# A new place on ScalarE for 100 weight negations and 8 weight casts, and another buffer order for the gate's weights

## The chip, the cores and the metric

The kernel is one program on one core of a Trainium2 chip. The metric is the device time of one execution in microseconds. Before the change it is 2661.06 us, the median of 3 runs (2660.25 to 2668.28).

## The reference, cut to what matters

The kernel computes two layers of a decoder trunk for one sequence of 1024 tokens, width 1024, in float32.

```python
def reference(x, ...):
    h = x
    for layer in range(DEPTH):                       # DEPTH = 2
        gains = norm_gains[layer]
        hn = rmsnorm(h, gains[0])
        if layer % 2 == 0:
            mix = mixer_ab(hn, w_in_ab[0], ...)      # gated DeltaNet + mLSTM, one output projection
        else:
            mix = mixer_c(hn, positions, w_qkv_c[0], ...)  # attention in a window of 128
        h = h + rmsnorm(mix, gains[1])
        hn = rmsnorm(h, gains[2])
        ff = jnp.square(jax.nn.relu(hn @ w_up[layer])) @ w_down[layer]   # 1024 -> 4096 -> 1024
        h = h + rmsnorm(ff, gains[3])
        gate = jax.nn.sigmoid(h @ w_ple_gate[layer])
        h = h + gate * (p[layer] @ w_ple[layer])
    return h
```

`rmsnorm` divides by the root of the mean square over the 1024 channels, so it needs a sum over the partitions. Inside the mixers each head projects q, k, v (and gates), and `mixer_c` scores 128 queries at a time against 256 keys.

## The kernel before

**Layout and weights.** Activations lie as channels by tokens, in two halves of 512 tokens (`h` = 0, 1; HT = 512). A matmul multiplies a 128 x 128 piece of a weight with 128 x 512 of activations. To keep float32 precision, every weight block of 128 x 8 x 128 is held as two float32r tiles, a high and a low half (names end in h and l), and a product is three matmuls: high by high, high by the activation's low half, low by high (lines 109 to 111 in `mm3`, lines 831 to 833 in `product`). One block by one half of the tokens is 24 matmuls.

The two halves are made by `wsplit` in three steps: POOL issues a DMA that loads the high half; ScalarE writes the negative of what landed into the low half (line 102, called the *negation* here); POOL issues a second DMA that adds the weight from memory onto it (line 103). So the low half is complete one negation and one transfer after the high half has landed. `raw_block` does it without the second transfer: a plain load, a cast on ScalarE, a subtraction on VectorE (`split`, line 145).

**Buffers.** Blocks from the pool "w" have 4 buffers for high and 4 for low halves. In the MLP's pool a tag "wd" has 8 buffers of either kind; `block` takes "w" where the index modulo 8 is under 4, else "wd". PSUM has 3 banks for the blocks ("mm"), 2 each for "s1" and "s2", 1 for "s3". The small tiles of the tag "sq" have 4 buffers.

**Order.** A scheduler orders the list of each engine by its own cost estimates when the program is built; every engine then works through its list in order, and an instruction whose input is not there holds up all that stand behind it on that engine.

**The stages of a layer, with the names that are used later:**

- *Projections of the mixer.* Layer 0: `proj` makes 28 blocks, each used for both halves of the tokens (48 matmuls). Layer 1: `roped` and `project` make 24 blocks named pq and pv, each used for one half (weights wqq000 and on, wqk01, wv10), with the scores of attention between them (ps and sc, lines 1193 and 1200). Their evictions are four copies on ScalarE (line 1103, tiles rs), the casts of q come at line 1109, the sum of the rotated parts at line 1133.
- *Output projection* (`out_proj`): 8 blocks wo00 to wo07 (layer 1: wo10 to wo17), first for half 0, then for half 1. Product mo, eviction into mix, a square moq, a running sum mos on VectorE (line 759). While half 1 is being multiplied, half 0 is normalized twice: pn00ps and mr00ps are matmuls with a matrix of ones that sum the squares over the partitions (`rstd`, line 116). The squares for mr00ps are mn00q (line 133, ScalarE), and their running sum is mn00s (lines 138 and 140, VectorE). The first digit is the layer, the second the half of the tokens.
- *MLP up* (`up`): 16 blocks wa00 to wa015 (layer 1: wa10 to wa115), a scheme of Strassen's kind that saves one product in eight. Block p gives product pa (4 of the 8 pieces), copied by ScalarE to sp and stored to s_dram, and product pb; their sum c gets a Relu and a square on ScalarE (lines 844 and 845) and is stored to r_dram, both stores issued by ScalarE (lines 846, 858). Blocks 12 to 15 are raw blocks. The squares of half 1 (mn01q) and the sums pn01ps and mr01ps lie among the first blocks. Then come further products from recombined weights (A, S).
- *MLP down*: products dn, in several groups; it ends with the layer's last norm.
- *Gate* (`ple`): 8 blocks wg000 to wg007 (half 0; also layer 1: wg100 and on), product pg, eviction a Tanh.

These are the lines of the split, of which everything here speaks:

```python
nc.gpsimd.dma_start(out=hi, in_=src)
nc.scalar.mul(lo, hi.bitcast(F32), -1.0)
nc.gpsimd.dma_start(out=lo, in_=src, accum_op=ALU.add)
```

Of the kernel before, what the change touches and what calls it, by code (L numbers as in the profile page):

```python
# [56 lines left out]
class Trunk:  # L57
    def __init__(self, ctx, tc, io):
        self.ctx, self.tc, self.nc, self.io = ctx, tc, tc.nc, io
        nc = self.nc  # L60
        self.cp = ctx.enter_context(tc.tile_pool(name="cp", bufs=1))
        self.bigp = ctx.enter_context(tc.tile_pool(name="bigp", bufs=4))
        self.wp = ctx.enter_context(tc.tile_pool(name="wp", bufs=4))
        self.dp = ctx.enter_context(tc.tile_pool(name="dp", bufs=1, space=DRAM))
        self.ps = ctx.enter_context(tc.tile_pool(name="ps", bufs=2, space=PSUM))
        cp = self.cp
        self.lead = self.ple_load(0, 0), self.ple_weight(0, 0)
        self.cst = cp.tile([P, C_HEAD], F32, name="cst")
        nc.sync.dma_start(out=self.cst, in_=io["cst"][:, 0:C_HEAD])
        self.par = cp.tile([P, G_N], F32, name="par")  # L70
        nc.sync.dma_start(out=self.par, in_=io["par"])
        self.row = cp.tile([P, R_N], F32, name="row")
        nc.sync.dma_start(out=self.row, in_=io["row"].partition_broadcast(P))
        self.ident = self.cst[:, C_ID:C_ID + P]
        self.ones = self.cst[:, C_ONE:C_ONE + P]
        self.epsc = cp.tile([P, 1], F32, name="epsc")
        nc.vector.memset(self.epsc, EPS)
        self.h_dram = self.dp.tile([2, 2, 2, P, KT, HT], F32, name="h_dram")
        self.pw_dram = self.dp.tile([2, 2, KT, P, HT], F32, name="pw_dram")
        self.mix_dram = self.dp.tile([KT, P, T], F32, name="mix_dram")  # L80
# [14 lines left out]
    def wsplit(self, src, tag, name, pool=None, n=KT, tags=None, **kw):  # L95
        nc = self.nc
        pool = pool or self.wp
        th, tl = tags or (tag + "h", tag + "l")
        hi = pool.tile([P, n, P], F32R, tag=th, name=name + "h", **kw)
        lo = pool.tile([P, n, P], F32R, tag=tl, name=name + "l", **kw)  # L100
        nc.gpsimd.dma_start(out=hi, in_=src)
        nc.scalar.mul(lo, hi.bitcast(F32), -1.0)
        nc.gpsimd.dma_start(out=lo, in_=src, accum_op=ALU.add)
        return hi, lo
# [220 lines left out]
    def proj(self, blk, hn, name):  # L325
        w = self.wsplit(self.io["w_in"][blk], "w", name)
        out = []
        for h in range(2):
            ps = self.mmps(f"{name}{h}")
            self.mm3(ps, w, hn[h])  # L330
            out.append(ps)
        return out
# [14 lines left out]
    def conv_silu(self, pool, out, ps, ch, name):  # L347
        nc = self.nc
        x = pool.tile([P, T], F32, tag="pre", name=name + "x", bufs=3)
        for h in range(2):  # L350
            nc.scalar.copy(x[:, h * HT:(h + 1) * HT], ps[h])
# [159 lines left out]
    def head_a_gate(self, pool, hd, hn):  # L511
        nc = self.nc
        n = f"a{hd}"
        gate = pool.tile([P, T], F32, tag="gate", name=n + "gate", bufs=2)
        for h, ps in enumerate(self.proj(hd * 4 + 3, hn, n + "z")):
            g = gate[:, h * HT:(h + 1) * HT]
            nc.scalar.activation(g, ps, AF.Tanh, scale=0.5)
            nc.vector.scalar_tensor_tensor(g, g, 1.0, ps, ALU.add, ALU.mult)
        return gate
# [49 lines left out]
    def head_b_in(self, pool, hd, hn):  # L569
# [5 lines left out]
        for dst, blk, s in ((kq[:, 0, :], 1, 1.0), (kq[:, 1, :], 0, P ** -0.5), (vT, 2, 1.0)):  # L575
            for h, ps in enumerate(self.proj(base + blk, hn, f"{n}{blk}")):
                nc.scalar.activation(dst[:, h * HT:(h + 1) * HT], ps, AF.Copy, scale=s)
        gate = pool.tile([P, T], F32, tag="gate", name=n + "gate", bufs=2)
        for h, ps in enumerate(self.proj(base + 3, hn, n + "og")):
            nc.scalar.activation(gate[:, h * HT:(h + 1) * HT], ps, AF.Tanh, scale=0.5)  # L580
# [139 lines left out]
    def block(self, mp, i, src, name):  # L720
        if i % 8 < 4:
            return self.wsplit(src, "w", name)
        return self.wsplit(src, "wd", name, pool=mp, tags=("wd", "wd"), bufs=8)

    def raw_block(self, mp, src, name, pool, tags, **kw):
# [4 lines left out]
        self.split(hi, lo, raw)  # L730
        return hi, lo

    def out_proj(self, src, w, layer, old, bias):
# [7 lines left out]
        def step(h, c):  # L741
# [4 lines left out]
            if h == 0:  # L746
                wts.append(self.block(mp, c, w[c], f"wo{layer}{c}"))
            ps = self.mmps(f"mo{layer}{h}{c}")
            self.mm3(ps, wts[c], src[h])
            if bias is None:  # L750
                nc.scalar.copy(acc[:, c, :], ps)
            else:
                nc.scalar.activation(acc[:, c, :], ps, AF.Identity, bias=bias[:, c:c + 1])
# [81 lines left out]
    def up(self, mp, layer, x11, x21, n1, later):  # L835
# [13 lines left out]
        for p in range(NP):  # L849
            if p < NP - 4:  # L850
                w = self.block(mp, p, wu[p], f"wa{layer}{p}")
            else:
                w = self.raw_block(mp, wu[p], f"wa{layer}{p}", mp, ("wd", "wd"), bufs=8)
# [3 lines left out]
            nc.scalar.copy(s, ps)  # L857
# [128 lines left out]
    def ple(self, mp, layer, acc, n0):  # L986
# [12 lines left out]
        for h in range(2):  # L999
            a = acc[h]  # L1000
            for c in range(KT):
                n = f"{layer}{h}{c}"
                if h == 0:
                    wts.append(self.block(mp, c, self.io["w_gate"][layer, c], "wg" + n))
# [5 lines left out]
                nc.scalar.activation(th, ps, AF.Tanh, scale=0.5)  # L1010
# [60 lines left out]
    def mixer_c(self, hn, norm, proj):  # L1071
# [5 lines left out]
        with tc.tile_pool(name="att", bufs=1) as pool:  # L1077
# [16 lines left out]
            def roped(h, blk, dst, name):  # L1094
                sl = slice(h * HT, (h + 1) * HT)
                w = self.wsplit(self.io["w_qkv"][blk], "w", "wq" + name)
# [4 lines left out]
                for b in range(4):  # L1101
                    o, i = slice(32 * b, 32 * b + 32), slice(32 * (b ^ 1), 32 * (b ^ 1) + 32)
                    nc.scalar.copy(xs[o], ps[i])
# [8 lines left out]
            def project(h, kt):  # L1112
# [9 lines left out]
                w = self.wsplit(self.io["w_qkv"][10 + kt], "w", f"wv{h}{kt}")  # L1122
# [3 lines left out]
                nc.scalar.activation(x, ps, AF.Identity, bias=self.par[:, G_BQKV + 10 + kt:G_BQKV + 11 + kt])  # L1126
# [211 lines left out]
```

## Time and profile before

| what | value |
|---|---|
| median of 3 runs | 2661.06 us (2660.25 to 2668.28) |
| the profiled execution | 2662.71 us |
| its span (first to last instruction) | 2660.9 us |
| mean granted clock of TensorE in it | 0.978 of full speed |
| TensorE matmuls (PE), weight loads (PEld) | 94%, 76% of the span |
| VectorE, ScalarE, POOL | 55%, 39%, 11% |
| memory traffic | 150 GB/s over the span |

All durations are from one execution, which took 1.65 us more than the median. A time in a row is in us from the start of the span. In a row of waits or in brackets behind an instruction, the name behind the arrow is what the waiting instruction was released by, as the profile infers it. A matmul row may stand for several instructions (x2). "PEclk" is the granted clock of TensorE in a stretch, 1.00 for full speed.

### The profile page before, as it was taken

The numbers are of one execution on the slowest core, as the hardware profiler recorded it, in microseconds if no ns is written. First come the engines' busy times: TensorE is split into PE (matmuls) and PEld (weight loads), VectorE is DVE, ScalarE is ACT, GpSimd is POOL, SyncE is SP. The second block draws the span as 40 slices with busy tenths as digits, with TensorE's granted clock in tenths as the row PEclk, the third lists the DMA queues.
The fourth block names the chain that finished last, engine by engine and source line by source line (L and its number), as shares of the span: only waits on it lengthen the run. The fifth ranks groups of instructions, "written<-read, shape, count | busy, mean of one in ns | idle before, by whom it ended". The sixth has DMA issues, their size and how long they took to land.

```text
span 2660.9 us, 31154 instructions
## 1 busy us (share of the span) xinstructions
PE 2502.4 (94%) x11541; PEld 2018.9 (76%) x11541; DVE 1466.9 (55%) x2768; ACT 1050.5 (39%) x1986; POOL 298.8 (11%) x405
## 2 busy tenths in 40 slices
PE   6999999999879999999999989968899999999999
PEld 4778878877668887888877766736678887888877
DVE  4788763252667763233366677763578751333373
ACT  5343333253465444211134666633465443211141
POOL 2111111111100001111021211001100000111120
PEclk9999999999989999999999999988999999999999
DMA  8443444466876457555445754216875456655543
GB/s 245 100 98 88 103 107 115 112 181 153 241 248 214 162 166 206 145 140 153 117 125 145 188 129 96 64 52 170 233 233 206 155 166 184 152 142 143 123 130 111
DMA packets 137223, 401.77 MB, mean 151 GB/s; under 512 B 24944, under 2 KB 25840, under 8 KB 132720
## 3 DMA queue, kind: packets, MB, share of 16 engines
q0 software_dynamic: 53920, 188.90, 31.8%
q1 hardware_dynamic: 51024, 166.84, 18.1%
q10 hardware_dynamic: 32128, 44.05, 4.6%
q8 instruction: 91, 1.49, 0.2%
q14 instruction: 60, 0.49, 0.1%
HBM read 321.16 MB, written 78.58 MB: 150 GB/s over the span
## 4 chain that ended last, share of the span: by engine, by line
PE 56%; issue 11%; DMA 6%; DVE 3%; ACT 2%; POOL 2%; POOLq 0%; SPq 0%; ACTq 0%; DVEq 0%
PE dn L831 8%; PE dn L833 8%; PE dn L832 8%; PE S L833 3%; PE S L831 3%; PE S L832 3%; PE pg L111 2%; PE pg L110 2%; PE pg L109 2%; PE po L1222 2%; PE mo L111 1%; PE mo L110 1%; PE mo L109 1%; PE A L833 1%; PE A L831 1%
## 5 line engine op out<-in xcount | busy, mean ns | idle before, releaser
L953 DVE TENSOR_TENSOR ff<-ff,dn 128x512 f32<-128x512 f32 x224 | 150.8, 684 | 318.1 <-PE dn L833 318.0
L831 PE MATMUL S<-xt,h 128*128 128x512 f32 x384 | 149.4, 389 | 0.0
L832 PE MATMUL S<-xt,h 128*128 128x512 f32 x384 | 149.4, 389 | 0.0
L833 PE MATMUL S<-xt,l 128*128 128x512 f32 x384 | 149.1, 389 | 0.0
L940 DVE TENSOR_TENSOR hid<-hid 128x1024 fp32r<-128x1024 f32 x64 | 75.8, 1221 | 125.5 <-ACT hid L939 125.5
L939 ACT CAST hid<-hid 128x1024 fp32r<-128x1024 f32 x64 | 64.2, 1045 | 96.7 <-DMA hid<-r_dram 77.4
L844 ACT ACTIVATE c<-c 128x512 f32<-128x512 f32 x64 | 40.3, 630 | 113.6 <-DVE c L917 88.0
L832 PEld LDWEIGHTS S<-xt,h 128*128 128x128 f32 x384 | 72.1, 188 | 15.0
L833 PEld LDWEIGHTS S<-xt,l 128*128 128x128 f32 x384 | 72.1, 188 | 15.0
L831 PEld LDWEIGHTS S<-xt,h 128*128 128x128 f32 x384 | 72.1, 188 | 14.9
L759 DVE TENSOR_TENSOR mos<-mos,moq 128x512 f32<-128x512 f32 x28 | 19.3, 688 | 92.8 <-ACT moq L755 92.6
L1209 ACT ACTIVATE sc<-sc,sm 128x128 f32<-128x128 f32 x128 | 49.8, 390 | 50.8 <-DVE sm L1206 36.3
L1222 PE MATMUL po<-pt,vt 128*128 128x512 f32 x120 | 61.1, 634 | 7.4 <-DVE pt L1220 4.1
L882 ACT CAST h<-r 128x1024 fp32r<-128x1024 f32 x32 | 33.6, 1050 | 73.5 <-DVE r L881 38.7
L1193 PE MATMUL ps<-kh,q 128*128 128x256 f32 (+1 forms) x128 | 38.7, 328 | 17.6 <-DVE sc L1200 10.7
L1013 DVE SCALAR_TENSOR_TENSOR pth<-pth,ppw 128x512 f32<-128x512 f32 x32 | 21.6, 687 | 56.4 <-ACT pth L1010 53.5
L831 PE MATMUL A<-xt,h 128*128 128x512 f32 x128 | 49.8, 389 | 0.0
L832 PE MATMUL A<-xt,h 128*128 128x512 f32 x128 | 49.8, 389 | 0.0
L833 PE MATMUL A<-xt,l 128*128 128x512 f32 x128 | 49.8, 389 | 0.0
L831 PE MATMUL S<-xb,s 128*128 128x512 f32 x128 | 49.8, 389 | 0.0
L832 PE MATMUL S<-xb,s 128*128 128x512 f32 x128 | 49.8, 389 | 0.0
L833 PE MATMUL S<-xb,s 128*128 128x512 f32 x128 | 49.8, 389 | 0.0
(3068 smaller groups left out, 7764.4 us busy)
## 6 DMA issues: line engine op xcount, KB each, us to landing
r<-w_up SPq DMA_DIRECT2D x64, 512.0 KB, 4.7
hid<-r_dram SPq DMA_DIRECT2D x32, 1024.0 KB, 7.9
r_dram<-c ACTq DMA_DIRECT2D x64, 256.0 KB, 2.9
pw_dram<-pwo SPq DMA_DIRECT2D x16, 512.0 KB, 3.8
h_dram<-mix SPq DMA_DIRECT2D x16, 512.0 KB, 4.4
s_dram<-sp ACTq DMA_DIRECT2D x32, 256.0 KB, 4.1
s<-s_dram SPq DMA_DIRECT2D x32, 256.0 KB, 2.8
r_dram<-s ACTq DMA_DIRECT2D x32, 256.0 KB, 4.7
```

The lines of the kernel that those rows point to most:

```text
L109: mm(ps, w[0][:, k, :], a[0][:, k, :], start=k == 0, stop=False)
L110: mm(ps, w[0][:, k, :], a[1][:, k, :], start=False, stop=False)
L111: mm(ps, w[1][:, k, :], a[0][:, k, :], start=False, stop=k == n - 1)
L831: mm(ps, wh, x[0][:, k, :], start=k == 0, stop=False)
L832: mm(ps, wh, x[1][:, k, :], start=False, stop=False)
L833: mm(ps, wl, x[0][:, k, :], start=False, stop=k == 3)
L844: nc.scalar.activation(x, x, AF.Relu)
L939: nc.scalar.copy(t[:, k:k + 2, :], raw[:, k:k + 2, :])
L940: tt(t[:, 4 + k:6 + k, :], raw[:, k:k + 2, :], t[:, k:k + 2, :].bitcast(F32), ALU.subtract)
L953: tt(a, a, ps, ALU.add)
L1209: nc.scalar.activation(sc[:, i, :], sc[:, i, :], AF.Exp, bias=nm[:, i:i + 1], scale=0.125, accum_out=den[:, i:i + 1])
L1222: mm(po, vt[:, jl + b, 64 * kv:64 * kv + P], pt[:, b].rearrange("p i t -> p (i t)"), start=kv == 0 and b == 2 - ns, stop=kv == 1 and b == 1)
```

## The change

`mark` notes an instruction that evicts a block. `behind(steps)` names the eviction noted `steps` marks ago, and the negation written inside it is queued on ScalarE behind that eviction: it is an edge in the order, not a wait on data, and the scheduler may still queue it later than that. With it, the place of the negation no longer comes from the scheduler's estimates alone. It is set for:

- `proj`: behind the eviction 3 blocks back, as soon as more than 3 marks exist (28 blocks);
- `out_proj`: 3 back (16 blocks in both layers);
- `up`: 5 back (24 negations, and the cast of the 8 raw blocks; `raw_block` has the split written out for that);
- the gate: 3 back from block 4 on (8 blocks);
- `roped` and `project`: 3 back (24 blocks).

The down blocks get none. In the gate, blocks 2 and 3 now take buffers of "wd" and blocks 4 and 5 buffers of "w". Tiles, transfers and arithmetic are the same in number and kind.

```diff
+    def mark(self, ins):
+        self.marks.append(ins.ins)
+
+    def behind(self, steps):
+        return nullcontext() if steps is None else self.tc.issue_after(self.marks[-steps])
+
+    def wsplit(self, src, tag, name, pool=None, n=KT, tags=None, late=None, **kw):
         nc = self.nc
         pool = pool or self.wp
         th, tl = tags or (tag + "h", tag + "l")
         hi = pool.tile([P, n, P], F32R, tag=th, name=name + "h", **kw)
         lo = pool.tile([P, n, P], F32R, tag=tl, name=name + "l", **kw)
         nc.gpsimd.dma_start(out=hi, in_=src)
-        nc.scalar.mul(lo, hi.bitcast(F32), -1.0)
+        with self.behind(late):
+            nc.scalar.mul(lo, hi.bitcast(F32), -1.0)
         nc.gpsimd.dma_start(out=lo, in_=src, accum_op=ALU.add)
...
-        w = self.wsplit(self.io["w_in"][blk], "w", name)
+        w = self.wsplit(self.io["w_in"][blk], "w", name, late=3 if len(self.marks) > 3 else None)
...
-            nc.scalar.copy(x[:, h * HT:(h + 1) * HT], ps[h])
+            ins = nc.scalar.copy(x[:, h * HT:(h + 1) * HT], ps[h])
+            if h == 0:
+                self.mark(ins)
...
-    def block(self, mp, i, src, name):
+    def block(self, mp, i, src, name, late=None):
         if i % 8 < 4:
-            return self.wsplit(src, "w", name)
-        return self.wsplit(src, "wd", name, pool=mp, tags=("wd", "wd"), bufs=8)
-
-    def raw_block(self, mp, src, name, pool, tags, **kw):
+            return self.wsplit(src, "w", name, late=late)
+        return self.wsplit(src, "wd", name, pool=mp, tags=("wd", "wd"), late=late, bufs=8)
+
+    def raw_block(self, mp, src, name, pool, tags, late=None, **kw):
         nc = self.nc
         raw = mp.tile([P, KT, P], F32, tag="wd", name=name + "r", bufs=8)
         nc.sync.dma_start(out=raw, in_=src)
         hi, lo = (pool.tile([P, KT, P], F32R, tag=t, name=f"{name}{j}", **kw) for j, t in zip("hl", tags))
-        self.split(hi, lo, raw)
+        with self.behind(late):
+            nc.scalar.copy(hi, raw)
+        nc.vector.tensor_tensor(lo, raw, hi.bitcast(F32), ALU.subtract)
         return hi, lo
...
-                wts.append(self.block(mp, c, w[c], f"wo{layer}{c}"))
+                wts.append(self.block(mp, c, w[c], f"wo{layer}{c}", 3))
             ps = self.mmps(f"mo{layer}{h}{c}")
             self.mm3(ps, wts[c], src[h])
             if bias is None:
-                nc.scalar.copy(acc[:, c, :], ps)
+                self.mark(nc.scalar.copy(acc[:, c, :], ps))
             else:
-                nc.scalar.activation(acc[:, c, :], ps, AF.Identity, bias=bias[:, c:c + 1])
+                self.mark(nc.scalar.activation(acc[:, c, :], ps, AF.Identity, bias=bias[:, c:c + 1]))
...
             if p < NP - 4:
-                w = self.block(mp, p, wu[p], f"wa{layer}{p}")
+                w = self.block(mp, p, wu[p], f"wa{layer}{p}", 5)
             else:
-                w = self.raw_block(mp, wu[p], f"wa{layer}{p}", mp, ("wd", "wd"), bufs=8)
+                w = self.raw_block(mp, wu[p], f"wa{layer}{p}", mp, ("wd", "wd"), 5, bufs=8)
             ps = self.mmps(f"pa{layer}{p}")
             self.product(ps, [x[:, 0:4, :] for x in w], x11)
             s = self.tp.tile([P, HT], F32, tag="sq", name=f"sp{layer}{p}", bufs=4)
-            nc.scalar.copy(s, ps)
+            self.mark(nc.scalar.copy(s, ps))
...
-                    wts.append(self.block(mp, c, self.io["w_gate"][layer, c], "wg" + n))
+                    wts.append(self.block(mp, (0, 1, 4, 5, 2, 3, 6, 7)[c], self.io["w_gate"][layer, c], "wg" + n,
+                                          3 if c > 3 else None))
...
+                self.mark(nc.scalar.activation(th, ps, AF.Tanh, scale=0.5))
...
-                w = self.wsplit(self.io["w_qkv"][blk], "w", "wq" + name)
+                w = self.wsplit(self.io["w_qkv"][blk], "w", "wq" + name, late=3)
...
-                    nc.scalar.copy(xs[o], ps[i])
+                    ins = nc.scalar.copy(xs[o], ps[i])
+                self.mark(ins)
...
-                w = self.wsplit(self.io["w_qkv"][10 + kt], "w", f"wv{h}{kt}")
+                w = self.wsplit(self.io["w_qkv"][10 + kt], "w", f"wv{h}{kt}", late=3)
```

The first place is ScalarE in the second half of the output projection of layer 0, where half 0 gets its second norm. The squares mn00q are the input of the sum mn00s; mo and mix are the projection's blocks. Line numbers of after are 8 to 21 higher for the same code (133 is 141, 102 is 110). Before:

```order
L133 ACTIVATE mn00q_5532<-mix_5189 128x512
L133 ACTIVATE mn00q_5535<-mix_5189 128x512
L102 ACTIVATE wa01l<-wa01h 128x1024
L133 ACTIVATE mn00q_5538<-mix_5189 128x512
L133 ACTIVATE mn00q_5541<-mix_5189 128x512
L751 COPY mix_5471<-mo_5585 128x512
L755 ACTIVATE moq_5611<-mix_5471 128x512
L102 ACTIVATE wa02l<-wa02h 128x1024
L133 ACTIVATE mn00q_5544<-mix_5189 128x512
L133 ACTIVATE mn00q_5547<-mix_5189 128x512
```

After:

```order
L141 ACTIVATE mn00q_5541<-mix_5189 128x512
L769 COPY mix_5471<-mo_5585 128x512
L773 ACTIVATE moq_5611<-mix_5471 128x512
L141 ACTIVATE mn00q_5544<-mix_5189 128x512
L141 ACTIVATE mn00q_5547<-mix_5189 128x512
L769 COPY mix_5471<-mo_5614 128x512
L141 ACTIVATE mn00q_5550<-mix_5189 128x512
L773 ACTIVATE moq_5640<-mix_5471 128x512
L141 ACTIVATE mn00q_5553<-mix_5189 128x512
L110 ACTIVATE wa00l<-wa00h 128x1024
L769 COPY mix_5471<-mo_5643 128x512
L110 ACTIVATE wa01l<-wa01h 128x1024
```

Two negations (wa01l, wa02l) stood among the eight squares; now the eight squares meet none (the first three stand straight ahead of the rows shown), and the negations of wa00 and wa01 follow the last of them.

The second place is ScalarE in the first blocks of the MLP of layer 0, around the negation of wa07 (sp is the copy of a block's first product, c the tile that gets Relu and square, mr01y the root for the second half's norm). Before:

```order
L857 COPY sp_5824<-pa_5811 128x512
L858 DMA s_dram_5805<-sp_5824 128x512
L102 ACTIVATE wa07l<-wa07h 128x1024
L844 ACTIVATE c_5840<-c_5840 128x512
L120 ACTIVATE pn01y<-pn01ps,epsc 128x512
L845 ACTIVATE c_5840<-c_5840 128x512
L846 DMA r_dram_5804<-c_5840 128x512
L857 COPY sp_5917<-pa_5904 128x512
```

After:

```order
L862 ACTIVATE c_6050<-c_6050 128x512
L128 ACTIVATE mr01y<-mr01ps,epsc 128x512
L863 ACTIVATE c_6050<-c_6050 128x512
L875 COPY sp_6182<-pa_6169 128x512
L864 DMA r_dram_5804<-c_6050 128x512
L876 DMA s_dram_5805<-sp_6182 128x512
L862 ACTIVATE c_6198<-c_6198 128x512
L110 ACTIVATE wa07l<-wa07h 128x1024
L863 ACTIVATE c_6198<-c_6198 128x512
```

The negation of wa07 stood behind the copy of a block before the sum pn01; it now stands behind mr01y and behind the Relu of block 5 (tile c_6198), two blocks before its use.

The third place is TensorE where block 7 of the same MLP begins (pa and pb are its two products, wa08h the next block's high half). Before:

```order
L831 MATMUL pa_6247<-x_5694,wa07h 128x512
L832 MATMUL pa_6247<-x_5694,wa07h 128x512
L833 MATMUL pa_6247<-x_5694,wa07l 128x512
L831 MATMUL pa_6247<-x_5694,wa07h 128x512
L832 MATMUL pa_6247<-x_5694,wa07h 128x512
```

After:

```order
L849 MATMUL pa_6247<-x_5694,wa07h 128x512
L850 MATMUL pa_6247<-x_5694,wa07h 128x512
L849 MATMUL pb_6263<-x_5703,wa07h 128x512
L850 MATMUL pb_6263<-x_5703,wa07h 128x512
L849 MATMUL pa_6286<-x_5694,wa08h 128x512
L850 MATMUL pa_6286<-x_5694,wa08h 128x512
L851 MATMUL pa_6247<-x_5694,wa07l 128x512
```

The matmuls with wa07l came third; now six with high halves alone are drawn ahead of the first of them.

## Rows read from the trace of the kernel before

**Rows 1.** The page, first part: busy us (share of the span) and instructions

```profile
PE 2502.4 (94%) x11541; PEld 2018.9 (76%) x11541; DVE 1466.9 (55%) x2768; ACT 1050.5 (39%) x1986; POOL 298.8 (11%) x405
```

**Rows 2.** Busy time of each engine by stretch; PEclk granted clock

```profile
130.00:520.00 390.00, 384.55 (x2287) 312.77 (x2286) 241.84 (x706) 136.28 (x383) 53.00 (x70) 1.00 0.44 103
660.00:740.00 80.00, 62.47 (x264) 49.89 (x262) 48.39 (x77) 33.53 (x54) 14.30 (x20) 0.91 0.89 251
1500.00:1680.00 180.00, 161.95 (x713) 122.47 (x712) 137.53 (x308) 129.13 (x312) 28.52 (x40) 0.93 0.53 116
1830.00:1925.00 95.00, 74.47 (x302) 58.86 (x301) 55.01 (x86) 41.16 (x65) 15.74 (x22) 0.89 0.86 242
```

**Rows 3.** Waits of TensorE: total us, times, longest

```profile
PE mr11ps L116 <- DVE mn11s L140: 10.7, 1, 10.7
PE mr01ps L116 <- DVE mn01s L140: 10.7, 1, 10.7
PE ps L1193 <- DVE sc L1200: 10.7, 2, 8.0
PE mr10ps L116 <- DVE mn10s L140: 9.8, 1, 9.8
PE mr00ps L116 <- DVE mn00s L140: 9.0, 1, 9.0
...
PE pqk L111 <- DMA wqk01l<-w_qkv: 4.7, 1, 4.7
...
PE pg L111 <- DMA wg002l<-w_gate: 3.0, 1, 3.0
...
PE pg L111 <- DMA wg102l<-w_gate: 2.9, 1, 2.9
...
PE pa L833 <- DVE wa012l L145: 2.7, 1, 2.7
```

**Rows 4.** Timeline of ScalarE from 648 us: start, us, instruction [idle before]

```profile
665.85 1.06 ACT L102 ACTIVATE wa01l<-wa01h 128x1024 fp32r<-128x1024 f32 x1 [3.81 <-DMA wa01h<-w_up]
...
677.85 1.06 ACT L102 ACTIVATE wa02l<-wa02h 128x1024 fp32r<-128x1024 f32 x1 [8.76 <-DMA wa02h<-w_up]
```

**Rows 5.** Timeline of VectorE in the same stretch

```profile
668.88 0.68 DVE L138 TENSOR_TENSOR mn00s<-mn00q,mn00q 128x512 f32<-128x512 f32 x1
669.48 0.68 DVE L759 TENSOR_TENSOR mos<-mos,moq 128x512 f32<-128x512 f32 x1
...
679.46 0.69 DVE L140 TENSOR_TENSOR mn00s<-mn00s,mn00q 128x512 f32<-128x512 f32 x1 [7.49 <-ACT mn00q L133]
```

**Rows 6.** Timeline of TensorE from 655 us

```profile
684.37 2.07 PE L116 MATMUL mr00ps<-mn00s,cst 128*128 128x512 f32 x2 [9.04 <-DVE mn00s L140]
...
687.52 0.42 PE L109 MATMUL mo<-mxh,wo05h 128*128 128x512 f32 x1
...
703.23 0.39 PE L831 MATMUL pa<-x,wa00h 128*128 128x512 f32 x1
...
708.68 1.02 PE L116 MATMUL pn01ps<-mos,cst 128*128 128x512 f32 x2
...
710.24 0.39 PE L831 MATMUL pa<-x,wa01h 128*128 128x512 f32 x1
```

**Rows 7.** DMA issues from 640 to 760 us: size, us to landing

```profile
r_dram<-c ACTq DMA_DIRECT2D x6, 256.0 KB, 4.2
...
wa07l<-w_up POOLq DMA_DIRECT2D x1, 512.0 KB, 5.4
...
wa010l<-w_up POOLq DMA_DIRECT2D x1, 512.0 KB, 8.3
```

**Rows 8.** Timeline of ScalarE at the start of attention

```profile
1508.70 2.35 ACT L1103 COPY rsq<-pqq 32x512 f32<-32x512 f32 x4
...
1560.22 1.06 ACT L102 ACTIVATE wqq100l<-wqq100h 128x1024 fp32r<-128x1024 f32 x1 [3.54 <-DMA wqq100h<-w_qkv]
```

**Rows 9.** Timeline of VectorE in the same stretch

```profile
1561.82 1.40 DVE L1133 TENSOR_TENSOR q<-rxq,q 64x512 fp32r<-64x512 f32 x2 [2.97 <-ACT q L1109]
```

More of the change, by code (lines that the diff above doesn't have):

```diff
@@ L1 @@
-from contextlib import ExitStack
+from contextlib import ExitStack, nullcontext
 import numpy as np
@@ L60, in __init__ @@
         nc = self.nc
+        self.marks = []
         self.cp = ctx.enter_context(tc.tile_pool(name="cp", bufs=1))
@@ L93, in mmps @@
         return self.psum("mm", name)
-    def wsplit(self, src, tag, name, pool=None, n=KT, tags=None, **kw):
+    def mark(self, ins):
[3 more added lines that the diff above has]
+    def wsplit(self, src, tag, name, pool=None, n=KT, tags=None, late=None, **kw):
         nc = self.nc
@@ L516, in head_a_gate @@
             g = gate[:, h * HT:(h + 1) * HT]
-            nc.scalar.activation(g, ps, AF.Tanh, scale=0.5)
+            ins = nc.scalar.activation(g, ps, AF.Tanh, scale=0.5)
+            if h == 0:
+                self.mark(ins)
             nc.vector.scalar_tensor_tensor(g, g, 1.0, ps, ALU.add, ALU.mult)
@@ L576, in head_b_in @@
             for h, ps in enumerate(self.proj(base + blk, hn, f"{n}{blk}")):
-                nc.scalar.activation(dst[:, h * HT:(h + 1) * HT], ps, AF.Copy, scale=s)
+                ins = nc.scalar.activation(dst[:, h * HT:(h + 1) * HT], ps, AF.Copy, scale=s)
+                if h == 0:
+                    self.mark(ins)
         gate = pool.tile([P, T], F32, tag="gate", name=n + "gate", bufs=2)
         for h, ps in enumerate(self.proj(base + 3, hn, n + "og")):
-            nc.scalar.activation(gate[:, h * HT:(h + 1) * HT], ps, AF.Tanh, scale=0.5)
+            ins = nc.scalar.activation(gate[:, h * HT:(h + 1) * HT], ps, AF.Tanh, scale=0.5)
+            if h == 0:
+                self.mark(ins)
         nc.gpsimd.tensor_scalar(gate, gate, 1.0, 1.0, ALU.mult, ALU.add)
@@ L1009, in ple @@
                 th = self.tp.tile([P, HT], F32, tag="sq", name="pth" + n, bufs=4)
-                nc.scalar.activation(th, ps, AF.Tanh, scale=0.5)
+                self.mark(nc.scalar.activation(th, ps, AF.Tanh, scale=0.5))
                 pw = self.tp.tile([P, HT], F32, tag="nt", name="ppw" + n)
@@ L1102, in roped @@
                     o, i = slice(32 * b, 32 * b + 32), slice(32 * (b ^ 1), 32 * (b ^ 1) + 32)
-                    nc.scalar.copy(xs[o], ps[i])
+                    ins = nc.scalar.copy(xs[o], ps[i])
+                self.mark(ins)
                 stt(x, ps, self.par[:, G_BQKV + blk:G_BQKV + blk + 1], cos[:, sl], ALU.add, ALU.mult)
@@ L1125, in project @@
                 x = pool.tile([P, 2, HT], F32, tag="pt", name=f"vx{h}{kt}", bufs=2)[:, 0, :]
-                nc.scalar.activation(x, ps, AF.Identity, bias=self.par[:, G_BQKV + 10 + kt:G_BQKV + 11 + kt])
+                self.mark(nc.scalar.activation(x, ps, AF.Identity,
+                                               bias=self.par[:, G_BQKV + 10 + kt:G_BQKV + 11 + kt]))
                 vx = x
```

## Prediction

> **What bounds the kernel now.** I read five views in this order. The page's first part says that TensorE is busy 94% of the span [rows 1]; all that any edit of order can win is in the other 6%, about 158 us. The stretches say where that is [rows 2]: in the first mixer TensorE works 384.55 of 390 us, so nothing is to be had there, while 660 to 740 us and 1830 to 1925 us, the end of the output projection and the start of the MLP in either layer, lose 17.5 and 20.5 us, and the attention stretch loses 18. The list of TensorE's waits names them [rows 3]: the four largest of one kind are mr00ps, mr01ps, mr10ps, mr11ps (9.0 + 10.7 + 9.8 + 10.7 = 40.2 us), the matmul that sums squares over partitions for the second norm; then two waits of the scores (10.7 together), and four for the low half of a weight.
>
> The releaser shown for mr is VectorE's running sum, but the cause is one engine further. VectorE itself waited 7.49 us for a square from ScalarE [rows 5], and ScalarE had two weight negations between the squares, wa01l and wa02l, which stood 3.81 and 8.76 us waiting for the first half of their weight to land [rows 4]. ScalarE does its list in order, so squares whose input was there waited behind a weight that is needed 25 us later. The scores' 8.0 us has the same shape: ScalarE waits 3.54 us in wqq100l, its q cast comes after, VectorE waits 2.97 us for that cast and only then reaches the copy that frees the score's bank [rows 8, 9].
>
> **The change part by part.** No arithmetic is added or taken away. 100 negations and 8 casts now have a place on ScalarE, with each negation goes the accumulating transfer that POOL issues after it, and POOL's list changes with them (first halves wa00 to wa03 now stand together, ahead of wa00l).
>
> *Negations out of the sums of squares.* In the new list the eight mn00 squares meet no negation. The eighth then waits only for the eviction of the third block before it and for the norm, which VectorE ends at 668.9. After that VectorE has ten adds, one each 0.60 us (668.88 to 669.48 [rows 5]): ready at 674.9. TensorE comes free for mr00 at 684.37 - 9.04 = 675.3 [rows 6]. The wait of 9.0 goes; what is late next is nothing, by 0.4 us. For mr01 the chain of norm, squares and sums is the same one, and four blocks of TensorE's work lie between pn01ps and mr01ps as between pn00ps and mr00ps, so it too comes just in time. I leave 0.5 us a layer for either being late: +1.0. What goes is 40.2; between 20 (VectorE keeps half, first rival) and 40.2.
>
> *Restart.* After such a wait matmuls start slowly: from mr00ps to the fourth matmul behind it is 3.15 us, from pn01ps, where nothing waited, 1.56 [rows 6]. The granted clock of that stretch is 0.91 [rows 2]: part of it at the lower level. So each wait costs 1.6 more; four make 6.4.
>
> *The new wait at wa07l.* This is the price. The negation of wa07 now stands behind the Relu of block 5, and TensorE's list pulls only six matmuls (1.4 us) ahead before it needs wa07l. A block is 24 matmuls and 5.45 us (703.23 to 708.68 [rows 6]). Block 5's Relu can run at the earliest 5.45 - 0.7 us before TensorE reaches block 7; but its buffer is one of four and is free only once the store of block 3's has landed (4.2 us [rows 7]), and that one starts late, behind the last square. Followed through, the Relu starts as TensorE reaches block 7. Then 0.63 + 1.06 for the negation [rows 4] + 0.1 to the issue + the transfer, 5.4 (wa07l) to 8.3 us (wa010l) [rows 7], less 1.4: 5.8 to 8.7 us. With the Relu as early as that it is 1.0. I take 6.3, near the quiet transfer, since the first halves have landed long before. With restart 7.9, two layers: +15.8.
>
> The Trainium skill, "DMA: Bandwidth & Descriptors", section "Anatomy of one DMA — SWDGE (gpsimd) path", puts such a transfer at about 2.0 us and bytes over 436 GB/s; for 512 KB that is, as an estimate from that page, 3.2 us. Rows 7 do not agree: 5.4 for this accumulating one when quiet. By the page the new wait would be some 3 us shorter in each layer, and the sum 5 to 6 us better.
>
> *Raw blocks 12 to 15.* The cast of wa012 now follows the Relu of block 11: 0.7 + 0.63 + 1.06 + 1.2 less 0.2 that the first two matmuls cover, 3.4 us, in place of 2.7 now at the same place and under a microsecond beside it [rows 3]. +0.6 for both layers; between -6 (it hides) and +4.
>
> *The gate's buffers.* Blocks 2 and 3 now take the buffers that come free while the last group of the MLP still runs; their halves are there before they are used. wg002l's 3.0 and wg102l's 2.9 go [rows 3]. Blocks 4 and 5 are loaded later: their negation follows the eviction three blocks back, 10.9 us ahead of use, against 0.6 + 1.06 + 0.1 + 5.4 to 8.3. This fits; +0.5 for block 5, whose negation stands behind two casts. Sum -5.4, bounds -6 and +2.
>
> *Attention.* wqk01l's 4.7 and the scores' 10.7 [rows 3] go with what held ScalarE up, and restarts of three of them, 4.8; also scores of the first query block now start some 40 us earlier among the projections. Against it, every low half is issued later. wqq003l: after the end of block q001 come four copies (2.35 us [rows 8]), the negation 1.06 and the transfer, 5.4 to 6.9 (half way to 8.3); TensorE is there after one block of 5.45 and has 1.3 us pulled ahead: a wait of 2.4 to 3.9, I take 3.2 and a restart. For wqq102l and wqq112l, which stand the same way but with transposes and products between, 1.5 each; 3 for places that I did not follow. +10.8 against -20.2: -9.4. Bounds: -20 and +40 (second rival).
>
> *The first mixer.* Negations move behind the eviction three blocks back, and a block there is 48 matmuls: over 20 us of lead against 8. TensorE stays full: 0, between -2 and +4.
>
> Sum: -40.2 - 6.4 + 1.0 + 15.8 + 0.6 - 5.4 - 9.4 = -44.0 us. The profiled execution took 2662.71, so 2618.7; the median is 1.65 below it: **2617**.
>
> **The rivals.**
> *The stall moves and is not won (2645).* If the squares only find their next wait, in VectorE's ten adds or in evictions that now stand between them, half of the mr waits and restarts stay, 23.3 us; and if the transfers of that stretch, whose engines are 0.89 busy [rows 2], take 8.3 us now that they are issued closer together, wa07l costs 2.4 more in each layer. -44.0 + 23.3 + 4.8 = -16: 2645. For it: the sum is in time by 0.4 us alone. Against it: ScalarE's waits [rows 4] were for single halves, and with them gone it has slack in that stretch.
>
> *Slower (2675).* The rule that the Trainium skill gives in "DMA: Bandwidth & Descriptors", section "Rules for kernel authors", is to issue a transfer early and wait late; this change waits late but issues the second half late. Here, as a mechanism of this kernel: in the 24 projection blocks of attention the low half of block b is started by the eviction of b - 3. The loop of three blocks is 5.45 + 2.35 + 1.06 + 0.1 + 5.4 to 8.3 = 14.4 to 17.3 us, against 16.35 of TensorE's work. If queueing on ScalarE (casts of the second norm, exponentials) adds 6.5 us to it, the loop is 21 to 24, each block loses 1.5 to 2.5, the stage 36 to 60, and the kernel stands at -44.0 + 9.4 + 36 to 60. It decides from 1.5 us a block on; at 2 us it is +13: 2675. Against it: attention's scores fill most blocks from the fifth on.
>
> *More (2601).* wa07l is not waited for, the Relu being early and the transfer quiet: -44.0 - 15.8 = -60. For it: the low end of that term is 1.0 us. Against it: four buffers serve two tiles a block.
>
> *The change does not do what it says:* ScalarE's list shows that it does; no chance given.
>
> **How the numbers follow.** Forecast 0.62 (own range 2606 to 2632), stall moves 0.16, more 0.14, slower 0.08. The range 2597 to 2648 leaves out the slower case and about the far third of the other two rivals, 0.2 in all. About 8 us (0.3%) is what a measurement can tell from no change: faster 0.89, same 0.05, slower 0.06.
>
> **What would show it.** Right: mr00ps to mr11ps gone from TensorE's waits or under 1 us each, granted clock near 1.0 in the two MLP starts; a wait of pa or pb for wa07l and wa17l of 4 to 8 us; wg002l and wg102l gone; ScalarE's waits for first halves (now up to 8.8) gone from the list, and wqq003l in place of wqk01l. Wrong: mr waits still over 4 us with VectorE waiting for squares; low halves in every second projection block; or wa08l to wa010l late as well, which would double the new wait.

## The result and the profile after

The changed kernel takes 2627.39 us (median of 4 runs, 2626.0 to 2629.07) against 2663.93 of the kernel before (4 runs); the ratio is 0.9878, 95% interval 0.9848 to 0.9909. 2617 was forecast, with a range of 2597 to 2648. The profiled executions stand at 2662.71 and 2627.19: 35.5 us less, where the sum said 44.0.

The two stretches at the end of the output projection and the start of the MLP, as in [rows 2]:

```profile
660.00:740.00 80.00, 75.35 (x324) 60.64 (x323) 62.49 (x98) 44.31 (x71) 15.06 (x21) 0.99 0.98 294
...
1830.00:1925.00 95.00, 88.27 (x370) 70.77 (x369) 69.72 (x111) 55.08 (x89) 14.88 (x20) 0.96 0.97 282
```

TensorE's idle time in these two stretches fell from 17.5 and 20.5 us to 4.7 and 6.7, and the granted clock rose from 0.91 and 0.89 to 0.99 and 0.96. The column before the last, the busy share of the transfer engines, is the one to keep in mind: it went from 0.89 and 0.86 to 0.98 and 0.97.

TensorE's waits, as in [rows 3]:

```profile
PE pqq L119 <- DMA wqq010l<-w_qkv: 5.3, 1, 5.3
PE pa L849 <- ACT wa112h L747: 5.3, 1, 5.3
...
PE pa L851 <- DMA wa17l<-w_up: 4.8, 1, 4.8
PE pa L851 <- DMA wa07l<-w_up: 4.4, 1, 4.4
...
PE pqq L119 <- DMA wqq000l<-w_qkv: 3.3, 1, 3.3
PE pa L849 <- ACT wa012h L747: 3.1, 1, 3.1
...
PE pqq L119 <- DMA wqq003l<-w_qkv: 2.8, 1, 2.8
PE pa L851 <- DMA wa011l<-w_up: 2.8, 1, 2.8
```

The four mr waits (40.2), the wait for wqk01l, the long one of the scores and those for wg002l and wg102l are gone; mr00ps is left with 0.22. In their place stand low halves, as forecast for wa07l, wa17l and wqq003l, and not as forecast for wqq010l, wqq000l and wa011l. For the casts wa012h and wa112h together with their low halves, 3.4 us in each layer were forecast; it is 3.6 in layer 0 and 5.3 in layer 1.

Where the time went is read from the starts of TensorE's first matmul in each stage. Before:

```profile
641.61 0.39 PE L109 MATMUL mo<-mxh,wo07h 128*128 128x512 f32 x1
755.66 0.39 PE L831 MATMUL pa<-x,wa07h 128*128 128x512 f32 x1
810.58 0.39 PE L831 MATMUL S<-xt,h 128*128 128x512 f32 x1
1478.65 0.39 PE L109 MATMUL pqk<-hn10h,wqk00h 128*128 128x512 f32 x1
1791.23 0.77 PE L109 MATMUL mo<-oh,wo14h 128*128 128x512 f32 x1 [7.71 <-issue]
1816.24 0.39 PE L109 MATMUL mo<-oh,wo17h 128*128 128x512 f32 x1
1932.66 0.39 PE L831 MATMUL pa<-x,wa17h 128*128 128x512 f32 x1
1985.32 0.39 PE L831 MATMUL S<-xt,h 128*128 128x512 f32 x1
```

After:

```profile
641.09 0.39 PE L117 MATMUL mo<-mxh,wo07h 128*128 128x512 f32 x1
732.26 0.39 PE L849 MATMUL pa<-x,wa07h 128*128 128x512 f32 x1
799.21 0.39 PE L849 MATMUL S<-xt,h 128*128 128x512 f32 x1
1465.35 0.39 PE L117 MATMUL pqk<-hn10h,wqk00h 128*128 128x512 f32 x1
1775.12 0.77 PE L117 MATMUL mo<-oh,wo14h 128*128 128x512 f32 x1 [8.64 <-issue]
1799.94 0.39 PE L117 MATMUL mo<-oh,wo17h 128*128 128x512 f32 x1
1891.22 0.39 PE L849 MATMUL pa<-x,wa17h 128*128 128x512 f32 x1
1957.31 0.39 PE L849 MATMUL S<-xt,h 128*128 128x512 f32 x1
```

The differences of these starts give the length of three stages, called squares, up and attention from here on; the same was done for the experiments (us, layer 0 / layer 1):

| kernel | squares: wo07h to wa07h | up: wa07h to first S | attention: wqk00h to wo14h |
|---|---|---|---|
| before | 114.0 / 116.4 | 54.9 / 52.7 | 312.6 |
| after | 91.2 / 91.3 | 67.0 / 66.1 | 309.8 |
| two late (9, 10) | 108.3 / 111.2 | 60.0 / 59.9 | 313.3 |
| four late (1, 2, 9, 10) | 99.0 / 98.8 | 61.4 / 59.7 | 310.3 |
| up seven | 91.2 / 91.3 | 64.1 / 66.8 | 309.8 |
| no add (8 to 11) | 91.2 / 91.2 | 56.3 / 57.2 | 310.2 |
| attention three | 91.2 / 91.3 | 65.2 / 65.5 | 298.2 |
| raw 8, POOL | 91.2 / 91.2 | 66.4 / 64.9 | 296.5 |
| last version | 91.2 / 91.3 | 65.6 / 65.5 | 296.8 |

The squares won 22.9 + 25.1 = 48.0 and up gave back 12.0 + 13.4 = 25.5. The first matmul with wo07h moves between 637 and 646 us from one kernel to the next, also where all ahead of it is the same; so single medians are compared with care, and stages are compared inside one trace. The experiments were timed in four rounds, in which the kernel before took 2662.9, 2657.31, 2654.98 and 2658.4 us, so kernels of different rounds are compared by their ratio to it.

### The profile page after: what moved, and what is told of

It is laid out like the page before. It is cut to its first block, busy times and chain, and to the rows that moved or that the text cites. A ratio compares the mean times of both kernels' runs of the same rounds, so it can differ in the third digit from the quotient of the medians.

```text
span 2625.4 us, 31145 instructions
## 1 busy us (share of the span) xinstructions
PE 2498.9 (95%) x11541; PEld 2019.3 (77%) x11541; DVE 1467.6 (56%) x2768; ACT 1050.4 (40%) x1986; POOL 299.4 (11%) x405
## 4 chain that ended last, share of the span: by engine, by line
PE 60%; issue 6%; DMA 6%; DVE 5%; ACT 2%; POOL 1%; SPq 0%; POOLq 0%; ACTq 0%; DVEq 0%
PE dn L849 8%; PE dn L850 8%; PE dn L851 8%; PE S L849 4%; PE S L851 4%; PE S L850 4%; PE pg L119 2%; PE pg L118 2%; PE pg L117 2%; DMA cx<-x_dram 2%; PE po L1243 1%; PE mo L119 1%; PE mo L117 1%; PE mo L118 1%; PE A L849 1%
## 5 line engine op out<-in xcount | busy, mean ns | idle before, releaser
L1029 ACT ACTIVATE pth<-pg 128x512 f32<-128x512 f32 x32 | 19.1, 598 | 92.9 <-PE pg L119 84.5
```

## The experiments

**Few negations.** Only the negations of up blocks 9 and 10 (first kernel) or 1, 2, 9 and 10 (second) get a place; proj, out_proj, gate, attention and the casts of the raw blocks are as in the kernel before.

```diff
-                w = self.block(mp, p, wu[p], f"wa{layer}{p}", 5)
+                w = self.block(mp, p, wu[p], f"wa{layer}{p}", 5 if p in (1, 2, 9, 10) else None)
```

> The kernel before, with a place (5 evictions back) for the negations of up blocks 9 and 10 alone, four in both layers; in ScalarE's list they leave the squares mn01q and mn11q, while wa01l and wa02l stay among mn00q. Theory A (squares queued behind a negation that waits for its first half are the whole stall): the waits of mr01ps and mr11ps go, 10.7 + 10.7 and two restarts of 1.6, those of mr00ps and mr10ps stay at 9 to 10: 2662.7 - 24.6 = 2638. Rival B (the gain at the start of the MLP comes from the other order and timing of all the loads, whose engines went from 0.89 to 0.98 busy): four negations of 100 change little, mr01ps stays over 7: 2655 to 2663.

Measured 2660.55, ratio 0.9999 [0.9978, 1.002].

> The kernel before, with a place for the negations of up blocks 1, 2, 9 and 10 alone, eight in both layers. Theory A: all four mr waits go (48 us by the changed kernel's trace at these stages), no wait for wa07l or wa17l, wa011l or wa111l comes: 2662.7 - 48 = 2615, faster than the changed kernel. Rival B: at least half of the gain stays away: 2638 or more.

Measured 2640.77, ratio 0.9924 [0.9899, 0.9949]. Both numbers lie in B's ranges, yet not for B's reason: mr01ps did not stay over 7 us, it waited 3.8 and 5.4. The stages tell it: with two, the squares got 5.7 and 5.2 us shorter, and up 5.1 and 7.2 longer, so that nothing was left. With four, the squares won 15.0 and 17.6, up lost 6.5 and 7.0. TensorE's waits with four, between 655 and 815 us:

```profile
PE pa L851 <- DVE wa012l L748: 8.5, 1, 8.5
PE mr01ps L124 <- DVE mn01s L148: 5.4, 1, 5.4
...
PE mr00ps L124 <- DVE mn00s L148: 0.2, 1, 0.2
```

And ScalarE there:

```profile
705.84 1.06 ACT L110 ACTIVATE wa06l<-wa06h 128x1024 fp32r<-128x1024 f32 x1 [7.23 <-DMA wa06h<-w_up]
...
715.53 1.07 ACT L110 ACTIVATE wa08l<-wa08h 128x1024 fp32r<-128x1024 f32 x1 [5.60 <-DMA wa08h<-w_up]
716.51 2.18 ACT L141 ACTIVATE mn01q<-mix 128x512 f32<-128x512 f32 x4
```

So A is right in kind: mr00ps goes by two negations, and what is left of mr01ps is two others (wa06l, wa08l) in front of the squares, which wait for their first half. But A missed that a new wait, 8.5 us for wa012l, takes part of it back.

**Up blocks from 7 on, 7 back.**

```diff
-                w = self.block(mp, p, wu[p], f"wa{layer}{p}", 5)
+                w = self.block(mp, p, wu[p], f"wa{layer}{p}", 5 if p < 7 else 7)
...
-                w = self.raw_block(mp, wu[p], f"wa{layer}{p}", mp, ("wd", "wd"), 5, bufs=8)
+                w = self.raw_block(mp, wu[p], f"wa{layer}{p}", mp, ("wd", "wd"), 7, bufs=8)
```

> The changed kernel, with up blocks 7 and later placed 7 evictions back in place of 5. Theory A: the new waits of TensorE at wa07l, wa011l and wa012h and their like in layer 1 come from negations that stand too far back in ScalarE's list; they go, 14.0 + 11.5 us between block 7 and the end of the pa and pb products: 2627 - 25.5 = 2602; up to 2608 if wa07l or wa08l, which now stand beside the squares of the second half, wait for their first half there. Rival C (those waits come from slow transfers, the engines being 0.97 to 0.98 busy in that stretch): the low halves come late all the same, 2619 to 2627.

Measured 2621.02, ratio 0.9847 [0.9817, 0.9877]. The waits for wa07l and wa011l went as A said, and the time did not: up is 64.1 and 66.8, against 67.0 and 66.1, and the interval overlaps that of the changed kernel. One wait in each layer has swallowed them:

```profile
PE pa L851 <- DVE wa112l L748: 12.5, 1, 12.5
PE pa L851 <- DVE wa012l L748: 12.1, 1, 12.1
```

VectorE, which makes wa012l, shows what is ahead of it (L787 scales by the norm of mr01ps; the combinations begin with cx):

```profile
731.86 5.39 DVE L787 SCALAR_TENSOR_TENSOR mix<-mix,par,mr01y 128x512 f32<-128x512 f32 x8
...
749.40 0.69 DVE L833 TENSOR_TENSOR cx<-mix,cx 128x512 f32<-128x512 f32 x1 [6.73 <-DMA cx<-x_dram]
...
767.44 1.24 DVE L748 TENSOR_TENSOR wa012l<-wa012r,wa012h 128x1024 fp32r<-128x1024 f32 x1
```

This is a chain that starts at mr01ps (717.0 us) and ends some 50 us later, 6.7 of it waiting for a load.

**Is it VectorE or the transfer?** First, blocks 12 and 13 without VectorE:

```diff
-            if p < NP - 4:
+            if p < NP - 2:
```

> The kernel with up blocks 7 and later placed 7 back, and now only up blocks 14 and 15 as raw blocks; blocks 12 and 13 get their low half by the accumulating transfer like all others, so VectorE no longer makes it. Theory E (with the squares free, TensorE runs into VectorE, which works through one unbroken list from the sum of mr01ps on: eight scalings, four groups of combinations, and only then the subtraction wa012l; the wait there was 12.1 and 12.5 us): the waits at block 12 go and TensorE comes to block 14 some 8 to 14 us earlier in each layer; half of it may be lost again at the next thing VectorE makes: 2621 - 16 = 2605, 2595 to 2612. Rival F (block 12 is late because its data come late, the transfer engines being full): two more accumulating transfers a layer make it worse, TensorE waits for the transfers of wa012l and wa013l: 2619 to 2635.

Measured 2624.34, ratio 0.9857 [0.983, 0.9885]. The wait for wa012l went, and up is 67.8 and 67.1: nothing won. TensorE now waits 5.8 us for a copy sp and 4.5 for the cast wa014h, both behind casts of the combinations on ScalarE. E is wrong as it was put. The number lies in F's range, but not for the transfer that F named: only 0.6 us was waited for a low half. It is the load of cx that came later still (VectorE waited up to 9.5 us for it). Taking off the subtraction alone, on POOL and beside the attention edit below:

> As the kernel of the three freed attention negations, with the raw blocks 12 to 15 as they were but their low half subtracted on POOL. It takes the subtraction alone off VectorE's list and no transfer away. Theory H: TensorE still runs into the late cx loads, the wait for wa012l (12.3 and 12.9) turns into waits for the copies sp or for wa013: 2614 to 2620. Theory E as it was put (VectorE's list alone is the bound): 2605.

Measured 2615.85, ratio 0.9851 [0.9811, 0.9892]: up 63.9 and 63.3, the wait again on a copy sp (5.2), as H said. Then the transfers, with the low half of blocks 8 to 11 left as the negative of the high half:

```diff
-        nc.gpsimd.dma_start(out=lo, in_=src, accum_op=ALU.add)
+        if name not in SKIP:
+            nc.gpsimd.dma_start(out=lo, in_=src, accum_op=ALU.add)
```

> The kernel with up blocks 7 and later placed 7 back; up blocks 8 to 11 leave out the accumulating transfer, so that their low half is only the negative of the high half: four transfers of 512 KB a layer less in the stretch where the engines are 0.98 busy, and everything else in place. VectorE waited there 6.7 us for the load of a combination's input (cx), and TensorE then 12.1 and 12.5 us for wa012l. Theory H (the next bound at the start of the MLP is the full transfer engines: the same bytes in less time): the cx wait goes, wa012l's waits fall to 5 or 6 us: 2621 - 13 = 2608. Rival I (the bound is the order on queues: cx is issued behind stores that wait for VectorE's scalings, and VectorE's list is one chain): the cx wait stays over 5 and wa012l over 10: 2617 to 2622.

Measured 2608.91, ratio 0.9825 [0.9785, 0.9866]. By ratio that is 6 us less than up seven, and the intervals overlap; it is the trace that decides. The same rows of VectorE, and TensorE's wait:

```profile
747.95 0.69 DVE L837 TENSOR_TENSOR cx<-mix,cx 128x512 f32<-128x512 f32 x1 [0.69 <-DMA cx<-x_dram]
...
760.60 1.22 DVE L752 TENSOR_TENSOR wa012l<-wa012r,wa012h 128x1024 fp32r<-128x1024 f32 x1
```

```profile
PE pa L855 <- DVE wa012l L752: 4.0, 1, 4.0
```

Up falls to 56.3 and 57.2, near what it was before the change. VectorE's waits for cx, both layers, in the changed kernel, up seven, the kernel with two more accumulating transfers a layer (blocks 12 and 13) and this one with four fewer:

```profile
DVE cx L833 <- DMA cx<-x_dram: 7.6, 2, 4.4
DVE cx L833 <- DMA cx<-x_dram: 13.7, 2, 7.0
DVE cx L833 <- DMA cx<-x_dram: 25.7, 4, 9.5
DVE cx L837 <- DMA cx<-x_dram: 1.4, 2, 0.7
```

The load that is late in up seven was issued at 737.65 us and took 11.7; the same one here was issued at 736.84 and took 4.8. So it was not issued late, as rival I has it, and H holds: with the squares free, the full transfer engines are the next bound there, by way of the late cx load.

**A version with fewer transfers.** Blocks 8 to 15 as raw blocks, subtracted on POOL, beside the attention edit below:

```diff
-            if p < NP - 4:
+            if p < 8:
...
-        nc.vector.tensor_tensor(lo, raw, hi.bitcast(F32), ALU.subtract)
+        nc.gpsimd.tensor_tensor(lo, raw, hi.bitcast(F32), ALU.subtract)
```

> The kernel of the three freed attention negations, with up blocks 8 to 15 as raw blocks and their low half subtracted on POOL: 4 transfers of 512 KB a layer less, and no subtraction on VectorE. Theory H with E (both full transfers and VectorE's list held TensorE there): waits at blocks 8 to 12 under 4 us in each layer, 2618 - 16 = 2602, 2594 to 2608. Rival I: TensorE waits as long for the copies sp behind ScalarE's casts of the combinations: 2614 to 2620. A third: POOL's subtraction is slow or takes VectorE's time, low halves come late one after the other: 2625 and more.

Measured 2619.6, ratio 0.9867 [0.9837, 0.9898]. It won nothing. The number is in I's range; the trace shows the third way at a smaller price, and I's way behind it. VectorE waited for no load of cx. Four subtractions held POOL from 729.6 to 740.7 us, and VectorE's eight scalings, 5.39 us above, took 13.96, so that the combinations began 6 us later. TensorE then waited 8.1 and 9.6 us for the casts wa013h and wa113h, which stand behind the combinations in ScalarE's list, and at most 1.0 for a low half from POOL. POOL and VectorE:

```profile
729.61 2.68 POOL L748 TENSOR_TENSOR wa08l<-wa08r,wa08h 128x1024 fp32r<-128x1024 f32 x1 [20.98 <-DMA wa010r<-w_up]
...
737.87 2.83 POOL L748 TENSOR_TENSOR wa011l<-wa011r,wa011h 128x1024 fp32r<-128x1024 f32 x1
```

```profile
729.28 13.96 DVE L787 SCALAR_TENSOR_TENSOR mix<-mix,par,mr01y 128x512 f32<-128x512 f32 x8
```

**Attention.** All 24 places taken away, then only three of them:

```diff
-                w = self.wsplit(self.io["w_qkv"][blk], "w", "wq" + name, late=3)
+                w = self.wsplit(self.io["w_qkv"][blk], "w", "wq" + name, late=None)
...
-                w = self.wsplit(self.io["w_qkv"][10 + kt], "w", f"wv{h}{kt}", late=3)
+                w = self.wsplit(self.io["w_qkv"][10 + kt], "w", f"wv{h}{kt}", late=None)
```

> The changed kernel, with the 24 projection blocks of attention put back to where the scheduler puts them. By the traces of before and after the attention stage moved by only 0.9 us. Theory A: two effects of some 20 us cancel: the waits for wqk01l (4.7) and of the scores (10.7) come back, those for wqq000l, wqq003l, wqq010l, wqq102l, wqq103l, wqq112l (14.8 together) go: 2627 to 2630. Rival D (the placement there is worth the 9.4 us that were forecast, and something else in attention got slower): 2636.

Measured 2630.08, ratio 0.9873 [0.9839, 0.9908]; attention takes 311.1 against 309.8, the waits of the scores (10.3) and for wqk01l (4.3) are back: A.

```diff
-                w = self.wsplit(self.io["w_qkv"][blk], "w", "wq" + name, late=3)
+                w = self.wsplit(self.io["w_qkv"][blk], "w", "wq" + name, late=None if name in ("q000", "q003", "q010") else 3)
```

> The kernel with up blocks 7 and later placed 7 back, and the place taken away from three negations in attention, wqq000l, wqq003l and wqq010l, for which TensorE waited 2.9 + 2.9 + 5.6 us; the other 21 keep theirs. TensorE's order goes back to scores behind the first twelve blocks. Theory A (those three negations stand too late; the scores' wait was ScalarE's q casts standing behind wv10l and wqq100l, which keep their new place): the three waits go and the scores do not wait long: 2621 - 11.4 - 3 restarts of 1.6 = 2605. Rival G (the scores ran without a wait only since they were spread among the first projections): a wait of the scores of some 10 us takes the place: 2616 to 2622.

Measured 2617.67, ratio 0.9839 [0.9814, 0.9863]. The stage is 11.6 us shorter (309.8 to 298.2), and the scores' wait that was 10.7 is 2.9, so G's wait of some 10 us did not come and A's mechanism holds in the stage. The six kernels that keep the changed kernel's places there took 305.1 to 310.2, the four with these three freed 296.5 to 298.2. The median lies in G's range all the same and gains only 3.4 us on up seven, with intervals that overlap: the profiled execution, 2610.42, is the shortest of its four. Part of the gain also goes to other low halves. TensorE's waits there:

```profile
PE pqq L119 <- DMA wqq112l<-w_qkv: 4.1, 1, 4.1
...
PE ps L1214 <- DVE sc L1221: 2.9, 2, 1.5
```

**Gate and first mixer undone,** each alone: the gate by `c` and `None` in its call, the mixer by `late=None` in `proj`.

> The changed kernel with the gate as before: its old buffer order and no place for its negations. From the sum forecast: the waits for wg002l and wg102l (3.0 and 2.9) come back, the gate stages (3.4 and 2.2 us shorter in the changed kernel) are as before: 2627 + 5.5 = 2633. Rival: those two stages got shorter by the earlier end of the MLP and not by the buffers: 2627.

Measured 2633.11, ratio 0.9911 [0.9881, 0.9942]; the waits are back at 2.6 (wg002l) and 2.4 (wg102l). The stages of the gate (from wg000h to wqk00h and from wg100h to the end) take 101.6 and 105.9 us, against 96.1 and 101.7 in the changed kernel. The forecast's reading holds in the stages; the interval overlaps that of the changed kernel. Whether the order of the buffers does it or the place of the negations is not shown, since both were undone together.

> The changed kernel with the 28 negations of the first mixer's projections put back to where the scheduler puts them. From the sum forecast (TensorE is full there either way): 2627, within 3 us, and the first block of the output projection at 599 to 601 us. Rival (the placement costs or wins time there that something later hid): the output projection starts 4 us or more earlier or later than in the changed kernel (601.3).

Measured 2623.33, ratio 0.9863 [0.9836, 0.9891]; the output projection starts at 597.9 against 601.3 us, no more than the spread told above. No effect of the 28 places is shown.

**The last version** joins up seven, attention three and no places in the first mixer.

> The version that the runs point to: up blocks 7 and later 7 back, three attention negations (wqq000l, wqq003l, wqq010l) without a place, and the 28 negations of the first mixer without a place as well, since taking those away alone cost nothing (2623 against 2627). By what the stages showed: 2617, a ratio to before of 0.983 to 0.985; the wait for wa012l stays at 12 in either layer, since no transfer is taken away. A rival: the first mixer's placement matters once the rest is fixed, 2622 to 2627.

Measured 2607.94 (5 runs), ratio 0.9817 [0.9791, 0.9843], just clear of the changed kernel's interval, and below the 0.983 that was expected, which lies inside its interval; its stages are those of attention three, and so is its profiled execution (2612.16 against 2610.42). The waits for wa012l and wa112l are still 12.1 and 12.2.

## Why the prediction was right, and where it was not

*Squares and restart, forecast -45.6, measured -48.0.* Right in cause and size: two negations of a layer alone took the wait of mr00ps away (four late). In the changed kernel mr00ps was ready with 0.22 us of waiting; "late next is nothing, by 0.4 us" was that close.

*wa07l, forecast 6.3 and a restart in each layer.* TensorE waited 4.4 and 4.8. ScalarE's rows after:

```profile
729.07 0.64 ACT L862 ACTIVATE c<-c 128x512 f32<-128x512 f32 x1 [0.95 <-DVE c L880]
729.60 1.04 ACT L110 ACTIVATE wa07l<-wa07h 128x1024 fp32r<-128x1024 f32 x1
```

The Relu came 3.2 us before TensorE reached block 7 (732.26), not with it, and the transfer took 7.2 us, not 5.4; the two partly cancel. But with that wait taken away (up seven) only 2.2 us of up came back in the two layers: another wait stood right behind it. The estimate of 3.2 us for such a transfer, from the Trainium skill's "DMA: Bandwidth & Descriptors", section "Anatomy of one DMA — SWDGE (gpsimd) path", is further off still; the measured 7.2 decides.

*"Raw blocks 12 to 15 ... +0.6", and wa07l as the only other new wait.* This is the step that failed. Up as a whole gave back 25.5 us where the terms for wa07l and the raw blocks gave 16.4. The two stretches of up, before:

```profile
755.66:810.58 54.92, 51.48 (x217) 41.48 (x216) 40.56 (x62) 34.27 (x56) 0.85 (x1) 0.97 0.73 241
1932.66:1985.32 52.66, 49.88 (x218) 40.31 (x217) 39.35 (x61) 33.11 (x53) 0.02 (x1) 1.00 0.75 244
```

After:

```profile
732.26:799.21 66.95, 56.15 (x218) 44.60 (x216) 39.38 (x60) 37.32 (x58) 3.47 (x4) 0.90 0.78 227
1891.22:1957.31 66.09, 54.35 (x218) 43.14 (x217) 39.80 (x60) 37.36 (x58) 3.49 (x4) 0.90 0.78 231
```

TensorE's idle time in up rose from 6.2 to 22.5 us, and its busy time, for the same matmuls, from 101.4 to 110.5, at a granted clock of 0.90 in place of 0.97 and 1.00. In layer 0 the granted clock stands at 0.50, the lower of its two levels (1.2 of 2.4 GHz), from 739.2 to 742.4, 763.1 to 769.7 and 776.7 to 779.9 us, at or just behind the waits for wa07l, wa011l and wa012h. Of the new 25.5 us, wa07l and wa17l are 9.2 (forecast 12.6), wa011l and wa111l 4.4 (no term), the raw blocks 2.8 (forecast 0.6; their waits went from 6.1 to 8.9), and the slower matmuls 9.1 (forecast 3.2, two restarts). So the waits behind wa07l and the slow matmuls that go with them were mis-sized, and a shorter wait at wa07l hid a part of it. In up seven the idle time is larger still, 27.5, but the busy time is 103.3: one long wait in each layer slowed the matmuls less than three shorter ones.

I followed the cast on ScalarE and did not ask what the same bytes in less time do. Four low halves are issued within 5 us of each other; the DMA rows of that stretch, after:

```profile
wa07l<-w_up POOLq DMA_DIRECT2D x1, 512.0 KB, 7.2
...
wa010l<-w_up POOLq DMA_DIRECT2D x1, 512.0 KB, 14.6
```

against 5.4 and 8.3 [rows 7]. Loads beside them come late too: VectorE waits 4.36 us for cx, ScalarE's casts of the combinations wait for VectorE, and the negation of wa011 and the cast of wa012 stand behind them. The rival "the stall moves" named this place's transfers, but priced them at wa07l alone.

*Attention, forecast -9.4, measured -2.8.* The gains came; the price was 14.8 us of waits for low halves, where the sum had 9.2 and one restart. (The stage took 310.3 to 313.3 in the kernels with the old places and 305.1 to 310.2 with the new ones, so the -2.8 is good to a few us.) I followed wqq003l (forecast 3.2, measured 2.8) and left wqq000l and wqq010l to "places that I did not follow". Their transfers were slow, 11.2 and 8.1 us where I had 5.4 to 6.9. Both were held on POOL's queue as well: the negation of wqq010l ended at 1518.3 us, and its transfer was issued at 1520.83, behind a load that waited for its buffer:

```profile
1520.31 0.53 POOL L108 DMA_DIRECT2D wqq013h<-w_qkv  x1 [4.89 <-PE pv L119]
1520.83 0.93 POOL L111 DMA_DIRECT2D wqq010l<-w_qkv  x1
```

*Gate, forecast -5.4:* the two waits went, 5.9, and the stages of the gate are 5.6 us shorter. *First mixer, forecast 0:* wo07h starts 0.5 us earlier. What is left, -4.1, lies in the MLP of layer 1 (from its first S to the gate 5.3 us shorter; in layer 0 it is 1.4 longer) and its cause stays open. No term of the sum had it, and without any edit there this stage takes 566.2 to 571.9 us over all the kernels; so the total came 4 us nearer to the forecast by luck.

Two readings in the prediction are off without weight in the sum: the weights behind wa01l and wa02l were needed 44 and 38 us later, not 25, and its own terms for wqq003l give a wait of 2.1 to 3.6 us, not 2.4 to 3.9.

The rival "slower", with late halves in every second attention block, did not come: six of 24 were waited for. "More" named the right wait to take away, wa07l, but up seven, which took it away, stood at 2621.02 and not at 2601.

## What to carry to other kernels

An engine that works in order should not meet an instruction that waits for a transfer ahead of work that a busier engine needs soon; look for it one engine behind the one that the wait names. When such a stall is taken away, price the stretch again with its bytes and its slowest chain in the shorter time: here 48 us were won and half of it was lost within the next 70 us, to waits behind transfers that had been hidden and to the slower matmuls between them. A rule applied at 108 places is a sum of wins and losses, and its places can be told apart: taking away 31 of them and moving others made it faster (ratio 0.9817 against 0.9878, the two intervals just apart).

## What the runs showed that I had not expected

An elementwise instruction on POOL stretches those of VectorE: eight scalings took 13.96 us beside four POOL subtractions (2.68 to 2.84 us each) and 5.39 without them. Four of the eight took 2.88 to 2.89 us each, the other four 0.74 to 0.75. The Trainium skill, "SBUF — State Buffer", section "SBUF: two separate sides", says that a VectorE instruction with two inputs in SBUF and a GpSimd instruction that reads SBUF hold one pair of ports in turn, each for its whole length; these rows agree with it.

The accumulating transfer of 512 KB took 5.1 us at best in the kernel before (5.4 in the stretch of [rows 7]) and up to 14.6 us in the changed kernel where four were issued within 5 us, in a stretch with the transfer engines 0.98 busy.
